# Other start addresses for the operand tiles of the second projections

## The chip, the cores and the metric

The kernel runs on one core of one Trainium2 chip. The metric is the time of one launch on the device, in microseconds. The kernel before was run three times: 2399.58, 2400.55 and 2401.14 us, median 2400.55 us.

## The reference

A small diffusion backbone in float32 takes 512 latent tokens and 256 context tokens (768 in all) of width 1024 through two layers. Each layer is a half-step SwiGLU, a token mixer (a gated short convolution in layer 0, grouped attention in layer 1) and another half-step SwiGLU. That makes six sub-layers. Each has an RMSNorm with a shift and a scale ahead, and a gated residual behind:

```python
def swiglu(h, w_in, w_out):
    gate, up = jnp.split(h @ w_in, 2, axis=-1)          # 1024 -> 2 x 2816
    return (jax.nn.silu(gate) * up) @ w_out             # 2816 -> 1024
def short_conv_mixer(h, w_in, w_conv, w_out):
    b_gate, c_gate, v = jnp.split(h @ w_in, 3, axis=-1)
    u = c_gate * v
    ...
    return (b_gate * y) @ w_out                         # 1024 -> 1024
```

The last product of each sub-layer, `... @ w_out`, is the **second projection**. Everything else is the first.

## The kernel before

**Layout.** Features lie on the 128 partitions and tokens along the free axis. A float32 operand is kept as two parts, high (`h`) and low (`l`), and a product is made of three matmuls (`mm3`, L875 to L878): high weights with high data (L876), high weights with low data (L877), low weights with high data (L878). So along a run of matmuls the moving operand goes high, low, high, high, low, high. Each matmul has its own weight load in front of it.

**First projections.** The SwiGLUs and the convolution compute most of them with Strassen-like products, seven per chunk of 128 features, on half the tokens each (384). Their data operands are the tiles `tB11`, `tB21`, `tB22`, `tT1` to `tT4`, each as `h` and `l`, in numbered slots. A product has 12 matmuls of 384 columns (4 blocks of 128 features, three matmuls each). The order of the products is fixed by `product_order`, and PE and SP follow the program's order.

**Second projections.** What the first projection of a chunk gives is split into `gh` and `gl` (ACT writes the high part, L205, VectorE the low part, L206). The SwiGLU takes its 22 chunks in six parts, one of two chunks and five of four (`FFN_PARTS`), the convolution its eight chunks in two parts of four. When a part is complete, `out_steps` (or, for the last part of the first three sub-layers, `out_close`) multiplies it into eight blocks of 128 output features. The tokens are taken as 512 and then 256, in `out_close` as 384 and 384. Over both groups a part of four chunks is 8 x 4 x 3 x 2 = 192 matmuls, and one of two chunks is 96.

**The tiles of the change.** `gated` (L1084, called by `g_of` and `z_of`) makes four tiles per part in the pool `g0`: tag `G0` holds the high parts of chunks 0 and 1, `G1` the high parts of chunks 2 and 3, `G2` the low parts of chunks 0 and 1, `G3` the low parts of chunks 2 and 3. One tile is two chunks of 768 float32 numbers, 6144 bytes per partition. Each tag has one buffer, which the next part fills again. A tag gets its place in the pool when it is first asked for. In the kernel before that happens in the boot, with a raw weight tile in `G0` and then weight tiles named `late` in `G2`, `G1` and `G3`, so the places stand in the order G0, G2, G1, G3. The pool `g0` serves the first four sub-layers (both SwiGLUs and the convolution of layer 0, the first SwiGLU of layer 1). The attention and the last SwiGLU have pools of their own.

Other users of these tags are `fT3` in `G1` and `fT4` in `G3` (sums that VectorE makes for the first projection) and the `late` weights of the boot. Behind `g0` in memory lie the pool `qp` (what the first projections give on the way to `gh` and `gl`) and the tiles `aw` of the modulation weights.

Of the kernel before, what the change touches and what calls it, by code (L numbers as in the profile page):

```python
# [10 lines left out]
F32 = mybir.dt.float32  # L11
# [7 lines left out]
P = 128  # L19
# [7 lines left out]
NH = NT // 2  # L27
# [106 lines left out]
def backbone(ctx: ExitStack, tc: tile.TileContext, a: dict, out: bass.AP):  # L134
# [25 lines left out]
    @contextmanager  # L160
    def psum(**tags):
        with ExitStack() as st:
            for tag, n in tags.items():
                pool = st.enter_context(tc.tile_pool(name=f"ps{tag}", bufs=n, space=PSUM))
                for t in tag:
                    bank[t] = pool, tag
            yield
# [1546 lines left out]
        return go  # L1714

    with tc.tile_pool(name="apool", bufs=1) as apool, tc.tile_pool(name="g0", bufs=1) as gp, tc.tile_pool(name="qp", bufs=1) as qp, psum(A=3, B=1, C=3, S=1):
        stage["ssq"] = lambda: apool.tile([P, 2, 512], F32, name="ssq", tag="acc").rearrange("p a b -> p (a b)")
        one, two = TOKENS

# [190 lines left out]
```

## Time and profile before

| what | value |
|---|---|
| median of three runs | 2400.55 us |
| the profiled execution | 2400.25 us |
| its span, first to last instruction | 2398.4 us |
| granted TensorE clock, mean | 0.998 |
| VectorE busy | 2031.9 us, 85% of the span |
| ScalarE (ACT) busy | 1166.3 us, 49% |
| GpSimd (POOL) busy | 135.4 us, 6% |
| DMA read from HBM | 249.16 MB |

A matmul is pipelined: the profile gives it a duration of about 390 ns for 512 columns, but the next one starts about 227 ns after it. So durations of matmuls are not the cost of one. What one costs in a run without gaps is the distance between two starts, which the timeline shows to 0.01 us. PEld is the weight load, which runs beside the matmuls. An address is given below as its remainder by 128 bytes.

### The profile page before, as it was taken

The numbers are of one execution on the slowest core, as the hardware profiler recorded it, in microseconds if no ns is written. First come the engines' busy times: TensorE is split into PE (matmuls) and PEld (weight loads), VectorE is DVE, ScalarE is ACT, GpSimd is POOL, SyncE is SP. The second block draws the span as 40 slices with busy tenths as digits, with TensorE's granted clock in tenths as the row PEclk, the third lists the DMA queues.
The fourth block names the chain that finished last, engine by engine and source line by source line (L and its number), as shares of the span: only waits on it lengthen the run. The fifth ranks groups of instructions, "written<-read, shape, count | busy, mean of one in ns | idle before, by whom it ended". The sixth has DMA issues, their size and how long they took to land.

```text
span 2398.4 us, 37639 instructions
## 1 busy us (share of the span) xinstructions
PE 2377.5 (99%) x14303; PEld 2252.4 (94%) x14303; DVE 2031.9 (85%) x4018; ACT 1166.3 (49%) x2198; POOL 135.4 (6%) x256
## 2 busy tenths in 40 slices
PE   9999999999999999999999999999999999999998
PEld 6999999999999999999999999999998889999998
DVE  6989989978988888888877988788778987987777
ACT  5634334355535553443435544343356776555555
POOL 0001111100000001000000001101100000000000
PEclk9999999999999999999999999999999999999999
DMA  9234444430334123323432144444441101233331
GB/s 337 86 113 139 129 127 131 129 115 27 107 105 132 40 70 116 119 95 117 128 105 67 51 130 129 142 139 120 136 132 54 45 10 58 70 121 96 99 106 62
DMA packets 93062, 253.71 MB, mean 106 GB/s; under 512 B 10320, under 2 KB 18640, under 8 KB 92880
## 3 DMA queue, kind: packets, MB, share of 16 engines
q1 hardware_dynamic: 71984, 183.65, 23.7%
q0 software_dynamic: 20352, 67.12, 9.5%
q8 instruction: 112, 1.84, 0.3%
q14 instruction: 70, 0.57, 0.1%
q10 hardware_dynamic: 544, 0.52, 0.1%
HBM read 249.16 MB, written 2.10 MB: 105 GB/s over the span
## 4 chain that ended last, share of the span: by engine, by line
PE 91%; DVE 4%; ACT 3%; DMA 1%; issue 1%; SPq 0%; DVEq 0%; ACTq 0%
PE ps_A L876 16%; PE ps_A L877 16%; PE ps_A L878 16%; PE ps_C L877 11%; PE ps_C L878 11%; PE ps_C L876 11%; PE ps_B L878 3%; PE ps_B L877 3%; PE ps_B L876 3%; PE ps_T L1557 1%; DVE f L778 0%; DMA ada<-in_ada_w 0%; DMA raw<-in_ffn_w_in 0%; ACT pr L1540 0%; PE ps_O L878 0%
## 5 line engine op out<-in xcount | busy, mean ns | idle before, releaser
L205 ACT ACTIVATE w<-raw 128x512 fp32r<-128x512 f32 (+1 forms) x862 | 522.4, 619 | 713.6 <-PE ps_A L878 222.6
L206 DVE TENSOR_TENSOR w<-raw,w 128x512 fp32r<-128x512 f32 (+1 forms) x862 | 574.0, 678 | 120.0 <-ACT w L205 106.3
L525 POOL DMA_DIRECT2D aw<-in_ada_t x240 | 129.4, 539 | 1367.0 <-DVE mods L546 968.5
L389 DVE TENSOR_TENSOR raw<-raw,raw 128x512 f32<-128x512 f32 x264 | 181.4, 688 | 10.0 <-DMA raw<-in_ffn_w_in 6.0
L877 PE MATMUL ps_C<-gl,w 128*128 128x512 f32 (+1 forms) x548 | 188.3, 344 | 0.0
L876 PE MATMUL ps_C<-gh,w 128*128 128x512 f32 (+1 forms) x548 | 188.1, 343 | 0.0
L878 PE MATMUL ps_C<-gh,w 128*128 128x512 f32 (+1 forms) x548 | 188.0, 343 | 0.0
L876 PE MATMUL ps_A<-gh,w 128*128 128x512 f32 (+1 forms) x540 | 185.5, 344 | 0.6 <-DVE x L944 0.6
L877 PE MATMUL ps_A<-gl,w 128*128 128x512 f32 (+1 forms) x540 | 185.6, 344 | 0.0
L878 PE MATMUL ps_A<-gh,w 128*128 128x512 f32 (+1 forms) x540 | 185.4, 343 | 0.0
L546 DVE CUSTOM_DVE_ANT_0 ps_S<-aw,silu_row,packed 128x512 f32<-128x512 f32 x208 | 156.8, 754 | 2.1 <-DMA aw<-in_ada_t 0.8
L546 DVE CUSTOM_DVE_ANT_0 ps_S<-aw,silu_row,mods 128x512 f32<-128x512 f32 x208 | 156.7, 753 | 1.0
L944 DVE SCALAR_TENSOR_TENSOR x<-ps_C,gat,x 128x512 f32<-128x512 f32 (+1 forms) x158 | 99.4, 630 | 44.0 <-PE ps_C L878 43.6
L876 PE MATMUL ps_A<-tB11h,w 128*128 128x384 f32 (+1 forms) x400 | 129.6, 324 | 0.2 <-ACT tB11h L800 0.2
L877 PE MATMUL ps_A<-tB11l,w 128*128 128x384 f32 (+1 forms) x400 | 129.3, 323 | 0.2 <-DVE tB11l L801 0.2
L878 PE MATMUL ps_A<-tB11h,w 128*128 128x384 f32 (+1 forms) x400 | 129.2, 323 | 0.0
L878 PE MATMUL ps_C<-tB22h,w 128*128 128x384 f32 (+2 forms) x376 | 121.6, 323 | 0.0
L877 PE MATMUL ps_C<-tB22l,w 128*128 128x384 f32 (+2 forms) x376 | 121.4, 323 | 0.0
L876 PE MATMUL ps_C<-tB22h,w 128*128 128x384 f32 (+2 forms) x376 | 121.3, 323 | 0.0
L944 DVE SCALAR_TENSOR_TENSOR x<-ps_A,gat,x 128x512 f32<-128x512 f32 (+1 forms) x162 | 101.7, 637 | 16.6 <-PE ps_A L878 16.4
L876 PEld LDWEIGHTS ps_A<-gh,w 128*128 128x128 f32 x540 | 102.2, 189 | 14.1 <-issue 1.0
L878 PEld LDWEIGHTS ps_C<-gh,w 128*128 128x128 f32 x548 | 103.8, 189 | 12.3
(486 smaller groups left out, 6938.7 us busy)
## 6 DMA issues: line engine op xcount, KB each, us to landing
raw<-in_ffn_w_in SPq DMA_DIRECT2D x170, 512.0 KB, 3.7
aw<-in_ada_t POOLq DMA_DIRECT2D x240, 256.0 KB, 2.9
raw<-in_ffn_w_out SPq DMA_DIRECT2D x80, 512.0 KB, 3.9
raw<-in_conv_w_in SPq DMA_DIRECT2D x24, 512.0 KB, 3.6
ada<-in_ada_w SPq DMA_DIRECT2D x28, 256.0 KB, 5.3
raw<-in_attn_w_qkv SPq DMA_DIRECT2D x12, 512.0 KB, 4.7
raw<-in_ada_w SPq DMA_DIRECT2D x8, 512.0 KB, 6.6
silu_row<-in_crow POOLq DMA_DIRECT2D x8, 512.0 KB, 4.1
```

The source lines that it names most:

```text
L205: hi = act.activation(dsth, src, AF.Copy)
L206: lo = dve.tensor_tensor(out=dstl, in0=src, in1=dsth.bitcast(F32), op=ALU.subtract)
L389: dve.tensor_tensor(out=quad(o), in0=quad(x), in1=quad(y), op=ALU.subtract)
L525: nc.gpsimd.dma_start(w, a["ada_t"][t, kh, j])
L546: ins = dve.tensor_tensor_reduce(out=junk, in0=w, in1=silu_row[kh][:, v, :], scale=1.0, scalar=total if kh else ada_b[:, i, hm // 2, col : ...
L876: pe.matmul(ps, wh, xh, start=first, stop=False, **kw)
L877: pe.matmul(ps, wh, xl, start=False, stop=False, **kw)
L878: pe.matmul(ps, wl, xh, start=False, stop=last, **kw)
L944: dve.scalar_tensor_tensor(out=x, in0=p[:, o - off : o - off + w], scalar=gat[:, m, v : v + 1], in1=x, op0=ALU.mult, op1=ALU.add)
L1557: pe.transpose(pt[:, c, :], pr[:, (c0 + c) * P : (c0 + c + 1) * P], ident)
```

## The change

Two lines are added ahead of everything that asks the pool `g0` for a tile:

```diff
     with tc.tile_pool(name="apool", bufs=1) as apool, tc.tile_pool(name="g0", bufs=1) as gp, ...
+        for tag, words in (("G0", 4 * NH + 16), ("G2", 4 * NH), ("G1", 4 * NH + 16), ("G3", 4 * NH)):
+            gp.tile([P, words], F32, name=f"place{tag}", tag=tag)
         stage["ssq"] = lambda: ...
```

`NH` is 384, so `4 * NH` words are the 6144 bytes of before. Two tags get 16 words (64 bytes) more than is used. Nothing reads or writes the placing tiles. The built program has the same instructions in the same order, with the same waits, on every engine; only the source lines behind L1716 move by two, and these start addresses differ:

| tile (bytes per partition) | start before, remainder by 128 | start now, remainder by 128 |
|---|---|---|
| `G0`: high parts of chunks 0, 1 | 184928, 96 | 184928, 96 |
| `G2`: low parts of chunks 0, 1 | 191072, 96 | 191136, 32 |
| `G1`: high parts of chunks 2, 3; `fT3` | 197216, 96 | 197280, 32 |
| `G3`: low parts of chunks 2, 3; `fT4` | 203360, 96 | 203488, 96 |
| tiles of `qp` and `aw` | | all 128 further up |

A chunk within a tile, and a token group within a chunk, begins a multiple of 128 bytes behind the tile's start, so the remainder of the tile holds for each matmul that reads it. All slots of the first projections, all weight tiles of the ring `w` and those held for the last part lie at remainder 96, before and now. Before, every moving operand of a second projection did too. Now the high and the low part of one chunk differ by 64.

One tile set of the kernel before has other remainders: in the first sub-layer `tB22` (and `tB12`) has rows of 386 numbers instead of 384 (two more columns for a shift), 1544 bytes, so that its four blocks of features begin at 96, 104, 112 and 120.

## The prediction

> **What bounds the kernel now.** I read the page first: the share of the engines, and the chain of work that ended last.
>
> ```profile
> span 2398.4 us, 37639 instructions
> ...
> PE 2377.5 (99%) x14303; PEld 2252.4 (94%) x14303; DVE 2031.9 (85%) x4018; ACT 1166.3 (49%) x2198; POOL 135.4 (6%) x256
> ...
> PE 91%; DVE 4%; ACT 3%; DMA 1%; issue 1%; SPq 0%; DVEq 0%; ACTq 0%
> ```
>
> PE is busy for 99% of the span and is 91% of the chain. Then the waits of PE, longest first:
>
> ```profile
> engine line waited for: us in total, times, longest us
> PE ps_C L500 <- DMA ada<-in_ada_w: 4.5, 1, 4.5
> PE ps_S L510 <- ACT adr L506: 0.9, 2, 0.6
> PE ps_T L1557 <- DVE p L206: 0.9, 3, 0.4
> PE ps_A L876 <- DVE x L944: 0.6, 1, 0.6
> ```
>
> The longest is 4.5 us in the boot. The one in a second projection (the last row) is 0.6 us, once, and no row names `gh` or `gl`. So the time is the number of matmuls times the distance between two starts, and only that distance is at stake. I therefore read the timeline of PE in a second projection of the first sub-layer, of which these are the first and last rows of two runs (start, duration, then the tiles):
>
> ```profile
> start us, us, engine line op out<-in xcount [idle before <-releaser]
> 245.24 0.39 PE L878 MATMUL ps_A<-gh,w 128*128 128x512 f32 x1
> ...
> 252.04 0.39 PE L878 MATMUL ps_A<-gh,w 128*128 128x512 f32 x1
> ...
> 252.62 0.28 PE L876 MATMUL ps_C<-gh,w 128*128 128x256 f32 x1
> ...
> 254.42 0.28 PE L876 MATMUL ps_C<-gh,w 128*128 128x256 f32 x1
> ```
>
> There are 30 steps from the first to the second row: 6.80 us / 30 = 226.7 ns for 512 columns. There are 15 steps from the third to the fourth: 1.80 / 15 = 120 ns for 256. The difference is 106.7 ns for 256 columns, so 0.417 ns per column. What is left, 120 - 106.7 = **13.3 ns, is a fixed part of each step**. The columns must be streamed whatever their address, unless the rate itself changes. So the fixed part is what a start address can most plausibly touch.
>
> **How many matmuls the change reaches.** This is counted from the loops and confirmed by a view of the stages that takes the instructions on `gh` alone:
>
> ```profile
> core 0: us, PE busy (x) PEld busy (x) DVE busy (x) ACT busy (x), PEclk, DMA share, GB/s
> 244.08:277.30 33.22, 31.13 (x128) 21.81 (x128) 0.56 (x1) 0.52 (x1) 1.00 0.40 120
> ```
>
> 128 matmuls on `gh` and so 64 on `gl` make the 192 of a part of four chunks. Three SwiGLUs with five such parts and one of 96, and the convolution with two parts, give 3 x (5 x 192 + 96) + 2 x 192 = 3552 matmuls. Of these, per four chunks, 64 read the high and 32 the low part of chunks 0 and 1, and as many those of chunks 2 and 3. Sorted by tile: 1280 stay in place (high, 0 and 1), 640 + 1088 = **1728 begin 64 bytes further up** (low of 0 and 1, high of 2 and 3), 544 begin 128 further up. At 1422 steps the remainder goes from 96 to 32 and at as many back, so 2844 steps lead between unlike remainders. Before there was none.
>
> **The cost of each part.** No instruction, wait or DMA is added, removed or moved, so everything depends on the price of an address. The trace has no operand moved by 64, so I bound the price by the nearest rows.
>
> First bound, from above. In the first sub-layer the rows of `tB22` are 8 bytes longer, and nine of the 12 matmuls of its product begin at remainders 104, 112 and 120 instead of 96. From one such product to the next lie seven products, 84 matmuls. I take three of these periods in the first sub-layer, and three in the second SwiGLU, where all begin at 96:
>
> ```profile
> 198.27 0.33 PE L876 MATMUL ps_C<-tB22h,w 128*128 128x384 f32 x1
> ...
> 241.99 0.33 PE L876 MATMUL ps_C<-tB22h,w 128*128 128x384 f32 x1
> ```
>
> ```profile
> 956.64 0.33 PE L876 MATMUL ps_C<-tB22h,w 128*128 128x384 f32 x1
> ...
> 1000.32 0.33 PE L876 MATMUL ps_C<-tB22h,w 128*128 128x384 f32 x1
> ```
>
> 43.72 against 43.68 us: 0.04 us for three products, 13.3 ns each, for 27 displaced matmuls **1.5 ns each** (0.7 to 2.2 with the rows' last digit). So an address does matter here, by little. For 1728 matmuls that is +2.6 us (at most 3.8).
>
> Second bound, from below. In the boot, one modulation product is computed from two groups of four weight tiles, the first at remainder 96 (`ada`), the second at 0 (`awb`):
>
> ```profile
> 46.01 1.06 PE L500 MATMUL ps_B<-ada,silu_p 128*32 128x512 f32 x8
> 47.01 0.45 PE L876 MATMUL ps_A<-tB21h,w 128*128 128x384 f32 x1
> ```
>
> ```profile
> 48.28 1.07 PE L500 MATMUL ps_B<-awb,silu_p 128*32 128x512 f32 x8
> 49.27 0.45 PE L876 MATMUL ps_A<-tB21h,w 128*128 128x384 f32 x1
> ```
>
> 1.00 us against 0.99 for eight records: -1.2 ns each, with the last digit from -3.7 to +1.2. At worst that is 1728 x -3.7 = -6.4 us. These matmuls are of another kind (32 weight columns, float32).
>
> The value I take is **nothing**. The second row, which moves by 32 bytes, gives nothing that its digits can tell. The first is nearer in kind, but its displacements are odd multiples of 8 bytes in two of three cases, and 1.5 ns would still be only 0.1% of the time.
>
> [...]
>
> The 544 matmuls moved by 128 keep their remainder: nothing. Bounded by the same 1.5 ns they cost 0.8 us. 72 matmuls of the boot whose weights lie in the `late` tiles at remainder 32 are worth 0.1 us at most.
>
> The writers of the moved tiles are ACT and VectorE, here VectorE's:
>
> ```profile
> L206 DVE TENSOR_TENSOR gl<-g,gh x158: 418/552/561, 122.9 to 2366.2; 128x384 fp32r<-128x384 f32 x118, 128x256 fp32r<-128x256 f32 x40
> ```
>
> Should a write take longer, 118 of 552 ns are 65 us in all, so 1% is 0.7 us, spread over four sub-layers and lying beside PE, which never waits for `gl` in the rows above. If that cover were gone, the 0.7 us would show. The tiles of `qp` and `aw` move by 128 and are read and written off PE's path; GpSimd, which loads `aw`, spends most of its time waiting for room:
>
> ```profile
> L525 POOL DMA_DIRECT2D aw<-in_ada_t x240 | 129.4, 539 | 1367.0 <-DVE mods L546 968.5
> ```
>
> The sum against the profiled execution is 2400.25 + 0. This run lies 0.3 us under the median of 2400.55, so I write 2400.5. Its own range, with the two bounds, is 2394 to 2404.5.
>
> **The rivals.**
>
> Slower: *a step between unlike remainders costs.* The 13.3 ns that a product on `tB22` takes longer may not come from nine displaced matmuls but from the one step per product that leads back, from 120 to 96. The change makes 1422 steps back, from 96 to 32 at a low part or the next chunk. At 13.3 ns they give 18.9 us: 2419.5. For it: the product has just one such step, and the excess is as large as the fixed part. Against it: three rows in the page of time cannot tell this from a cost spread over all nine. It decides from 4.8 / 1422 = 3.4 ns per step on.
>
> Faster: *high and low at the same remainder stand in each other's way, and the fixed part is the price.* Before, each operand begins at the same place as the one ahead of it and as the weights loaded beside it. If half of the 13.3 ns went at the 2844 unlike steps, that would be 6.7 x 2844 = 19.0 us: 2381.5. For it: the fixed part is there at every width, and every pair in the kernel is alike. Against it: nine displaced matmuls on `tB22` have weights at another remainder than their data, and took longer, not shorter.
>
> [...]
>
> That the change does not do what it says is excluded: the addresses in the built program differ as given, and nothing else does.
>
> **How the numbers follow.** About 0.2% (4.8 us) is what a measurement of this kernel can tell from no change. Forecast, no visible effect: 0.54. The slower rival, with a price per step anywhere from 3.4 to 13.3 ns: 0.28. The faster one, from 4.8 to 19 us: 0.18. I give the slower one more because the only displaced products in the trace are slower. The predicted time is 2400.5 us. For 8 in 10 the range must take in the forecast's 2394 to 2404.5 and, on each side, what leaves at most about a tenth: of the slower cases (4.8 to 19 us, evenly) those up to +14.5, leaving 0.09; of the faster ones those to -11.5, leaving 0.09. So 2389 to 2415.
>
> **What the changed profile would show.** The rows of the timeline at a second projection decide. If 30 steps at 512 columns are again 6.80 us and 15 at 256 again 1.80, the forecast is right. If the slower rival holds, the distances go up at the steps from 96 to 32 (high to low part in chunks 0 and 1, low to high in 2 and 3), by 13 ns at most, and the last sub-layer, whose pool did not move, stays as it is. If the faster rival holds, the same steps get shorter. In each case the product on `tB22` and the first projections keep their distances. A difference elsewhere, or PE waits on `gh` or `gl`, would say that my reading by PE alone is wrong; a streaming rate that changes with the address, with a loss that grows with the columns, would break the limit by the fixed part.

## The result and the profile after

| | median, us | lowest to highest | runs |
|---|---|---|---|
| before | 2400.32 | 2399.40 to 2401.14 | 22 |
| changed | 2403.37 | 2402.94 to 2404.11 | 22 |

The changed kernel takes 3.05 us longer, a ratio of 1.0013 with a 95% interval of 1.0008 to 1.0019. That is within 0.2%, but the two sets of runs don't overlap: it is slower. The prediction's 2400.5 us was 2.9 us too low, and its range of 2389 to 2415 held the time.

The page of the changed kernel, at the lines that the prediction showed of before:

```profile
span 2401.8 us, 37639 instructions
...
PE 2380.8 (99%) x14303; PEld 2249.8 (94%) x14303; DVE 2032.4 (85%) x4018; ACT 1165.9 (49%) x2198; POOL 135.0 (6%) x256
...
PE 90%; DVE 4%; ACT 3%; DMA 2%; issue 1%; SPq 0%; DVEq 0%; ACTq 0%
```

The span is 3.4 us longer and PE's busy time 3.3 us, with the same number of instructions everywhere. The waits of PE in the changed kernel are these:

```profile
PE ps_C L500 <- DMA ada<-in_ada_w: 4.7, 2, 4.5
PE ps_S L510 <- ACT adr L506: 1.0, 2, 0.7
PE ps_T L1557 <- DVE p L206: 0.9, 3, 0.4
...
PE ps_A L876 <- DVE x L944: 0.6, 1, 0.6
```

They are those of before to 0.2 us, again without `gh` or `gl`. So no wait of more than that was added, and what grew is the distance between matmuls that run without a gap. The timeline of PE in the changed kernel, at the four places that the prediction read (the same part of the first sub-layer, 30 steps from the first row to the second and 15 from the third to the fourth):

```profile
start us, us, engine line op out<-in xcount [idle before <-releaser]
245.55 0.39 PE L878 MATMUL ps_A<-gh,w 128*128 128x512 f32 x1
...
252.51 0.40 PE L878 MATMUL ps_A<-gh,w 128*128 128x512 f32 x1
...
253.10 0.28 PE L876 MATMUL ps_C<-gh,w 128*128 128x256 f32 x1
...
254.86 0.28 PE L876 MATMUL ps_C<-gh,w 128*128 128x256 f32 x1
```

At 512 columns 6.96 us / 30 = 232.0 ns, where it was 226.7. At 256 columns 1.76 / 15 = 117.3 ns, where it was 120. **One width got slower and the other faster.** A second place, in the second SwiGLU of layer 0, shows the same over whole runs. The rows are the first matmul at 512 columns, the first at 256, the next at 512, and the first of the product that follows the part; there are 36, 36 and 120 steps between them. Before:

```profile
910.80 0.39 PE L876 MATMUL ps_C<-gh,w 128*128 128x512 f32 x1
...
919.00 0.28 PE L876 MATMUL ps_C<-gh,w 128*128 128x256 f32 x1
...
923.32 0.40 PE L876 MATMUL ps_A<-gh,w 128*128 128x512 f32 x1
...
944.16 0.34 PE L876 MATMUL ps_A<-tB11h,w 128*128 128x384 f32 x1
```

Changed:

```profile
912.35 0.39 PE L876 MATMUL ps_C<-gh,w 128*128 128x512 f32 x1
...
920.68 0.28 PE L876 MATMUL ps_C<-gh,w 128*128 128x256 f32 x1
...
924.91 0.39 PE L876 MATMUL ps_A<-gh,w 128*128 128x512 f32 x1
...
945.85 0.34 PE L876 MATMUL ps_A<-tB11h,w 128*128 128x384 f32 x1
```

The first run of 512 went from 8.20 to 8.33 us, the first of 256 from 4.32 to 4.23, the whole part from 33.36 to 33.50. I measured every stage of both traces in this way, from its first matmul to the first of the next stage. The second projections of the first four sub-layers are 2.89 us longer in sum: +0.175 for each part of four chunks in the first sub-layer and +0.142 in the others. By width, the 2.89 us are +5.63 at 512 columns (1488 matmuls), +0.53 at 384 (576) and -3.28 at 256 (1488), which is +3.8, +0.9 and -2.2 ns per step: **the change gains at 256 columns and loses more than that at 512.** The last sub-layer is the same to 0.01 us. What remains of the 3.4 us is about 0.5, spread over many stages; the largest pieces are the attention (+0.15) and the boot (+0.13), and +0.018 stands in the first matmuls behind most parts.

### The profile page after: what moved, and what is told of

It is laid out like the page before. It is cut to its first block, busy times and chain, and to the rows that moved or that the text cites. A ratio compares the mean times of both kernels' runs of the same rounds, so it can differ in the third digit from the quotient of the medians.

```text
span 2401.8 us, 37639 instructions
## 1 busy us (share of the span) xinstructions
PE 2380.8 (99%) x14303; PEld 2249.8 (94%) x14303; DVE 2032.4 (85%) x4018; ACT 1165.9 (49%) x2198; POOL 135.0 (6%) x256
## 4 chain that ended last, share of the span: by engine, by line
PE 90%; DVE 4%; ACT 3%; DMA 2%; issue 1%; SPq 0%; DVEq 0%; ACTq 0%
PE ps_A L876 16%; PE ps_A L878 16%; PE ps_A L877 16%; PE ps_C L878 10%; PE ps_C L876 10%; PE ps_C L877 10%; PE ps_B L878 3%; PE ps_B L876 3%; PE ps_B L877 3%; DMA ada<-in_ada_w 1%; PE ps_T L1557 1%; DVE f L778 0%; DMA raw<-in_ffn_w_in 0%; ACT pr L1540 0%; PE ps_O L878 0%
## 5 line engine op out<-in xcount | busy, mean ns | idle before, releaser
L389 DVE TENSOR_TENSOR raw<-raw,raw 128x512 f32<-128x512 f32 x264 | 181.7, 690 | 8.8 <-DMA raw<-in_ffn_w_in 4.4
```

Source lines behind the costliest of these rows:

```text
L389: dve.tensor_tensor(out=quad(o), in0=quad(x), in1=quad(y), op=ALU.subtract)
```

## The experiments

Every address is told here by one number: **d, the start of the data tile less the start of the weight tile, in bytes, by its remainder by 256.** The weights that the second projections read begin at 96 by 256. Before, d is 0 for all four tiles. The table gives d in the order high and low of chunks 0 and 1, then high and low of chunks 2 and 3. "Part" is what a part of four chunks takes longer than before (33.34 us in the first sub-layer, 33.35 in the second SwiGLU of layer 0), and "sum" the same for all second projections of the first four sub-layers. Both are read from the traces. Each median is compared with that of the kernel before, run beside it (2400.32 us for the change, 2400.07 to 2400.10 for the others).

| kernel | d | median, us | ratio [95%] | part: first, later | sum |
|---|---|---|---|---|---|
| the change | 0, 64, 64, 128 | 2403.37 | 1.0013 [1.0008, 1.0019] | +0.175, +0.142 | +2.89 |
| `e1_all_at_32` | 64, 64, 64, 64 | 2397.65 | 0.9990 [0.9981, 0.9999] | -0.484, -0.065 | -2.72 |
| `e2_pairs_apart` | 0, 0, 64, 64 | 2402.27 | 1.0010 [1.0001, 1.0019] | +0.125, +0.124 | +2.16 |
| `e3_whole_lines` | 0, 128, 128, 128 | 2405.17 | 1.0021 [1.0013, 1.0030] | +0.195, +0.221 | +4.66 |
| `e4_lows_at_32` | 0, 64, 128, 192 | 2405.03 | 1.0021 [1.0012, 1.0030] | +0.302, +0.281 | +5.08 |
| `e5_everything_64` | 0, 0, 0, 0 | 2399.99 | 1.0000 [0.9991, 1.0009] | 0.00, 0.00 | 0.00 |
| `e6_long_rows_of_B22` | 64, 64, 64, 64 | 2394.23 | 0.9976 [0.9967, 0.9986] | -0.484, -0.500 | -6.74 |
| `e7_by_256` | 0, 0, 0, 0 | 2400.39 | 1.0001 [0.9992, 1.0010] | 0.00, 0.00 | -0.01 |
| `e8_all_by_128` | 128, 128, 128, 128 | 2408.49 | 1.0035 [1.0023, 1.0048] | +0.407, +0.441 | +8.07 |
| `e9_all_by_192` | 192, 192, 192, 192 | 2401.44 | 1.0006 [0.9997, 1.0015] | +0.346, -0.074 | +0.98 |
| `e10_late_T_64` | 64, 64, 64, 64 | 2391.05 | 0.9961 [0.9949, 0.9974] | -0.484, -0.500 | -6.75 |
| `e11_one_low_tile` | 0, 64, 0, 0 | 2402.30 | 1.0010 [1.0001, 1.0019] | +0.076, +0.049 | +1.89 |
| `e12_weights_moved` | 64, 64, 64, 64 (not in the last parts) | 2394.56 | 0.9976 [0.9966, 0.9986] | -0.049, -0.073 | -1.09 |
| `e13_change_long_rows` | 0, 64, 64, 128 | 2404.10 | 1.0017 [1.0008, 1.0027] | +0.175, +0.159 | +3.12 |
| `e14_lows_at_64` | 0, 64, 0, 64 | 2404.48 | 1.0018 [1.0009, 1.0026] | +0.258, +0.244 | +4.12 |

Split by width like the change, the sums of the other kernels have its two signs wherever d is not 0. At 512 and at 256 columns they are +2.00 and -4.73 us with all tiles at 64 (`e1_all_at_32`), +7.62 and -1.09 at 128, +8.15 and -7.61 at 192, +3.62 and -1.80 in `e2_pairs_apart`, +6.37 and -2.58 in `e14_lows_at_64`. So the two signs don't need a mixture of distances, and the time of a kernel is what is left of two larger numbers.

The expectations call the theories by letters. **A**: a step between unlike starts costs. **B**: each matmul whose data stand 64 away from the weights costs. **C**: the tiles behind the pool, which move too, cost. **D**: the distance d of each matmul sets its step, whatever its neighbours are. **E**: the start of the data counts by itself. **F**: the state in which a run is entered persists through it. **G**: neighbours with unlike d throw a run out of its even pattern. The later ones were formed when the earlier ones fell.

### Which part of the change costs

The four kernels of the first round differ from the change in the placing line alone. `e1_all_at_32` puts a pad ahead and moves all four tiles by 64, so that there is no unlike step left:

```diff
-        for tag, words in (("G0", 4 * NH + 16), ("G2", 4 * NH), ("G1", 4 * NH + 16), ("G3", 4 * NH)):
+        for tag, words in (("pad", 16), ("G0", 4 * NH), ("G2", 4 * NH), ("G1", 4 * NH), ("G3", 4 * NH)):
```

> All four operand tiles of the second projections (first four sub-layers) begin 64 bytes further up: every moving operand at remainder 32, none unlike its neighbour. Theory A (a step between unlike remainders has a price; the change has 2844 such steps for 3.05 us, 1.07 ns each): no such step, so as before, 2400.3 us, and in the timeline 6.80 us for 30 steps at 512 columns and 1.80 us for 15 at 256. Theory B (a moving operand at 32 beside weights at 96 has a price; the change has 1728 for 3.05 us, 1.77 ns each): all 3552 have it, +6.3 us, 2406.6.

Measured: 2397.65 us, 2.45 faster than before. A had 2400.3 and missed this gain. B fell: the most displaced kernel is the fastest of this round. Its rows in the second SwiGLU of layer 0:

```profile
909.44 0.39 PE L876 MATMUL ps_C<-gh,w 128*128 128x512 f32 x1
...
917.69 0.28 PE L876 MATMUL ps_C<-gh,w 128*128 128x256 f32 x1
...
921.93 0.39 PE L876 MATMUL ps_A<-gh,w 128*128 128x512 f32 x1
...
942.73 0.34 PE L876 MATMUL ps_A<-tB11h,w 128*128 128x384 f32 x1
```

8.25 us at 512 columns (+0.05) and 4.24 at 256 (-0.08): the same two signs as in the change, in another proportion.

`e2_pairs_apart` keeps high and low of a chunk together and moves chunks 2 and 3 by 64:

```diff
+        for tag, words in (("G0", 4 * NH), ("G2", 4 * NH + 16), ("G1", 4 * NH), ("G3", 4 * NH)):
```

> Chunks 0 and 1 at remainder 96 (high and low), chunks 2 and 3 at 32 (high and low). Theory A: unlike steps only from chunk to chunk, about 540 of them, +0.6 us, 2400.9. Theory B: 1632 matmuls at 32, +2.9 us, 2403.2, close to the change.

Measured: 2402.27 us, the sum +2.16, between what A (2400.9) and B (2403.2) gave. There are a fifth as many unlike steps as in the change (two per 12 matmuls of a part of four chunks, at most 2 x 272 = 544, against 2844), and three quarters of its loss. A single price per unlike step is out: 2.89 us / 2844 = 1.0 ns in the change, 2.16 / 544 = 4.0 ns here at the least.

`e3_whole_lines` moves all tiles but the first by 128, `e4_lows_at_32` each by 64 more than the one ahead:

```diff
+        for tag, words in (("G0", 4 * NH + 32), ("G2", 4 * NH), ("G1", 4 * NH), ("G3", 4 * NH)):
```

```diff
+        for tag, words in (("G0", 4 * NH + 16), ("G2", 4 * NH + 16), ("G1", 4 * NH + 16), ("G3", 4 * NH)):
```

> Low parts of chunks 0 and 1 and both tiles of chunks 2 and 3 move by 128 bytes, and what lies behind them too: every remainder by 128 is as before. Theories A and B: as before, 2400.3. If it is the moved tiles of qp and aw, or any move at all, that costs (theory C): as the change, 2403.4.

> High parts of all chunks at 96, low parts of all chunks at 32. Theory A: 2368 unlike steps (to each low part and back), +2.5 us, 2402.8. Theory B: 1184 matmuls at 32, +2.1 us, 2402.4. This run alone doesn't tell A from B by the time; by the timeline A lengthens the steps around the low part and leaves the one from high to high alone, B lengthens those of the low part alone.

Measured: 2405.17 and 2405.03 us. A and B missed both: they had 2400.3 for the first, and 2402.8 and 2402.4 for the second. In `e3_whole_lines` every remainder by 128 is as before, and yet it loses more than the change. Either it was the tiles behind the pool (C), or addresses count by more than 128.

### By what an address counts

Four kernels to tell C, D and E apart. `e5_everything_64` places nothing and moves everything, data and weights, by 64:

```diff
-SHIFT = 24
+SHIFT = 40
```

> The places of the change are gone, and instead every tile of the kernel in SBUF begins 64 bytes further up, weights and data alike, so that data and weights still begin at the same remainder by 256. Theory D (the distance between a data start and a weight start sets the step): as before, 2400.1 us, steps of 120, 173.3 and 226.7 ns. Theory E (the start of the data itself sets it): as with the four tiles at the new place, so steps near 230 ns at 512 columns and 113 to 118 at 256 in the second projections, and changed steps in the first projections as well.

`e7_by_256` is `e3_whole_lines` with 256 bytes for 128, and `e8_all_by_128` moves all four tiles by 128:

```diff
+        for tag, words in (("G0", 4 * NH + 64), ("G2", 4 * NH), ("G1", 4 * NH), ("G3", 4 * NH)):
```

```diff
+        for tag, words in (("pad", 32), ("G0", 4 * NH), ("G2", 4 * NH), ("G1", 4 * NH), ("G3", 4 * NH)):
```

> High parts of chunks 0 and 1 in place, the three other tiles 256 bytes further up. Theories D and E with a period of 256 bytes: as before, 2400.1 us, every distance in the timeline as before. If any unlike start costs whatever its size: as the run by 128 or the change, 2403 to 2405.

> All four tiles 128 bytes up, so that no two neighbours are unlike. In the run by whole 128 one tile stayed and three moved, +5.1 us. If unlike neighbours are the cause (theory A at a period of 256): as before, 2400.1. If the distance of data and weights sets the price (theory D): all 3552 matmuls pay what 2272 paid there, about +8 us, 2408.

Measured: 2399.99 us, 2400.39 and 2408.49. A common move does nothing, which speaks against E. A move by 256 does nothing, although the tiles behind the pool move by it, which speaks against C. (`e11_one_low_tile` below ends it: there too they stand 256 up, and it loses.) A move of all four tiles by 128 costs 8.4 us, with no unlike step in it, so A alone falls. The rows of `e7_by_256` and then of `e8_all_by_128`:

```profile
911.09 0.39 PE L876 MATMUL ps_C<-gh,w 128*128 128x512 f32 x1
...
919.29 0.28 PE L876 MATMUL ps_C<-gh,w 128*128 128x256 f32 x1
...
923.61 0.40 PE L876 MATMUL ps_A<-gh,w 128*128 128x512 f32 x1
```

```profile
915.14 0.40 PE L876 MATMUL ps_C<-gh,w 128*128 128x512 f32 x1
...
923.54 0.28 PE L876 MATMUL ps_C<-gh,w 128*128 128x256 f32 x1
...
927.82 0.40 PE L876 MATMUL ps_A<-gh,w 128*128 128x512 f32 x1
...
948.94 0.34 PE L876 MATMUL ps_A<-tB11h,w 128*128 128x384 f32 x1
```

8.20 and 4.32 us in the first, to the digit those of before. 8.40 and 4.28 in the second.

`e12_weights_moved` has the placing lines of `e1_all_at_32` and puts a tile of 48 words (192 bytes) ahead of the ring of weights. The weights move by 192. The four tiles, which lie behind the ring, move by 192 + 64 = 256, so that by 256 they begin where they did before. That makes d = 64 with the weights moved in place of the data:

```diff
+    wp.tile([P, 48], F32, name="placew", tag="placew", bufs=1)
```

> The data tiles begin at the remainders by 256 of before; the ring of the weights is moved by 192, so that data stand 64 above the weights in first and second projections alike (in the parts whose weights lie in slots, and the second projections of the last sub-layer, the distance is 0 as before). Theory D: the second projections as in the first run (parts of four -0.07 or -0.48 us), the products of 384 columns about as before (those parts of 384 columns did not change there), the products of 256 columns in the last sub-layer 113 to 118 ns instead of 120: 2386 to 2393. Theory E (the data's own start): as before, 2400.1.

Measured: 2394.56 us, less of a gain than D gave (2386 to 2393), but far from E's 2400.1. In the later sub-layers a part is 0.073 us shorter, where moving the data had given 0.065: with the data at their remainder of before, the weights alone do it. E is out, and in these kernels d by 256 is what an address counts by. Two things differ from `e1_all_at_32`, since the first projections read the same ring, while their data stand still, and get d = 64 too. The first sub-layer's parts gain 0.049 instead of 0.484, and in the last sub-layer each stage of 336 first-projection matmuls of 256 columns is 0.735 us shorter. Most of this kernel's gain lies there: 3.55 us in the first projections of the last sub-layer, against the sum of 1.09. Where the weights of a last part stand in slots, which didn't move, d is another. It stays 0 in those of the first three sub-layers and in three quarters of that of the fourth. In the last sub-layer it is 192, and the 132 matmuls of 256 columns that begin its last part are 0.868 us shorter, 6.6 ns each, as in the later sub-layers of `e9_all_by_192` below (113.5 ns for 119.8).

`e9_all_by_192` moves all four tiles by 192, with `("pad", 48)` for `("pad", 16)`:

> All four tiles 192 bytes up, none unlike its neighbour: the fourth distance of data and weights by 256 (0 is the kernel before, 64 gave -2.5 us, 128 gave +8.4). Theory D says only that the second projections of the first four sub-layers take another length and the last sub-layer the same; if the four distances lie on one wave, the one at 192 mirrors that at 64, some -2 us, 2398. Theory A: 2400.1.

Measured: 2401.44 us, a miss by 3.4. A distance of 192 is the mirror image of 64 only in the later sub-layers (-0.074 against -0.065). In the first it costs 0.346 where 64 gains 0.484. And the likeness of -0.074 and -0.065 is chance: the first run at 512 columns and the one at 256 behind it take 8.39 and 4.09 us here, 8.25 and 4.24 in `e1_all_at_32`.

### What the first sub-layer has

In `e1_all_at_32` a part gains 0.484 us in the first sub-layer and 0.065 in the others, at equal d. What differs is the product ahead of it: only in the first sub-layer does `tB22` have rows of 386 numbers. `e6_long_rows_of_B22` gives every sub-layer of that width such rows (the two more columns aren't multiplied):

```diff
+        if name == "B22" and geo.half == NH:
+            more = 2
...
-                    mm3(ps, wh[:, k, :], wl[:, k, :], xh[:, k, :], xl[:, k, :], kh == 0 and k == 0, kh == 1 and k == 3)
+                    mm3(ps, wh[:, k, :], wl[:, k, :], xh[:, k, : ps.shape[-1]], xl[:, k, : ps.shape[-1]], kh == 0 and k == 0, kh == 1 and k == 3)
```

> All four tiles 64 bytes up as in the first run, and tB22 gets its rows of 386 numbers in the next two sub-layers and the first SwiGLU of layer 1 too, where they were 384, so that the product ahead of each second projection is like that of the first sub-layer. In the first run a part of four chunks was shorter than before by 0.48 us in the first sub-layer, but by 0.07 in the two other SwiGLUs. Theory F (the state in which the run of matmuls is entered persists through it): the parts of the other SwiGLUs become shorter by 0.48 too where that product stands ahead of them, four per SwiGLU, -0.42 each, -3.3 us in all, against some +0.5 us for the products on the long rows: 2394.9. If the state is not carried over, they stay at -0.07 and the time is that of the first run or 0.5 above, 2397.7 to 2398.2.

Measured: 2394.23 us, 3.4 less than `e1_all_at_32`. A part of a later sub-layer gains 0.500, as the first one's do, for 0.047 us that the long rows cost in each stage of first projections ahead of it. Its rows (the lines of this kernel stand two further down):

```profile
908.44 0.39 PE L878 MATMUL ps_C<-gh,w 128*128 128x512 f32 x1
...
916.68 0.28 PE L878 MATMUL ps_C<-gh,w 128*128 128x256 f32 x1
...
920.76 0.39 PE L878 MATMUL ps_A<-gh,w 128*128 128x512 f32 x1
...
941.29 0.34 PE L878 MATMUL ps_A<-tB11h,w 128*128 128x384 f32 x1
```

The gain sits at 256 columns: 4.08 us for 36 steps, 113.3 ns, against 4.24 in `e1_all_at_32` with the same d and the same instructions in that run. So **what happened ahead of this run decided its steps**: F holds here. The run at 512 columns ahead of it hardly differs in length (8.24 us against 8.25). There the steps of the three matmuls that `mm3` makes are about 226, 229 and 232 ns in turn in both kernels, by the starts in the traces. In `e6_long_rows_of_B22` the 226 lies behind the first of the three, in `e1_all_at_32` behind the third, and in the first sub-layer of `e1_all_at_32`, where 256 columns take 113.3 ns too, behind the first again.

`e13_change_long_rows` puts the same edit on top of the change, since F could also be why the change loses:

> The change itself, and tB22 with rows of 386 numbers in all SwiGLUs and the convolution, as in the run that took -0.5 us off each part of four when all tiles stood at one distance. Theory G (unlike neighbours keep throwing the run out of its pattern, so nothing of the state at its entry lasts): the parts stay where the change has them, +0.14 to +0.18 us each, and the long rows cost some 0.9 us: 2404 to 2404.5. If the entry decides the pattern here too: parts some 0.4 us shorter, eight of them, 2401.

Measured: 2404.10 us, the later parts +0.159. The entry, which made 0.435 us a part at equal distances (-0.065 to -0.500), does next to nothing where distances are mixed (0.017 us a part).

### Whether the mixture costs

By D alone the change is the sum of its tiles. With the sums of the kernels whose tiles all have one d (64: -2.72 us, 128: +8.07, for 3552 matmuls), 1728 matmuls at 64 and 544 at 128 give -1.32 + 1.24 = -0.1 us, where +2.89 was measured. `e11_one_low_tile` leaves one tile at 64 and brings the others to 0, and `e14_lows_at_64` does so with both low tiles:

```diff
+        for tag, words in (("G0", 4 * NH + 16), ("G2", 4 * NH + 48), ("G1", 4 * NH), ("G3", 4 * NH)):
```

```diff
+        for tag, words in (("G0", 4 * NH + 16), ("G2", 4 * NH + 48), ("G1", 4 * NH + 16), ("G3", 4 * NH)):
```

> Only the low parts of chunks 0 and 1 stand 64 bytes off; the tiles of chunks 2 and 3 are 256 bytes up, which is as before. If each matmul pays by its own distance (theory D, summed): 640 of 3552 matmuls at 64, -0.4 us, 2399.7. If neighbours at unlike distances throw the run out of its even steps (theory G): 1280 unlike steps of the change's 2844, +1.4 us, 2401.5, all of it at chunks 0 and 1 and shortly behind them.

> Only two distances, alternating in every chunk: high parts 0, low parts 64 from the weights (chunks 2 and 3 lie 256 further up, which is as before). Theory D, summed over matmuls: 1184 at 64, -0.8 us, 2399.3. Theory G: twice the unlike steps of the run with one low tile, which had +2.2 us: about +4 us, 2404.

Measured: 2402.30 and 2404.48 us. D gave 2399.7 and 2399.3; G gave 2401.5 and about 2404. With d = 0 throughout the kernel takes 2400.1, with d = 64 throughout 2397.65, and with the two in turn 2404.48. **Of 0 and 64 neither costs, and their mixture does.** It does so at 512 columns, by 6.37 us against 0 and 2.00. At 256 the mixture (-2.58) lies between the two (0 and -4.73). G fits the place of the loss, at 512 columns, but not its size: a part of the later sub-layers loses five times as much in `e14_lows_at_64` as in `e11_one_low_tile`, not twice, and the matmuls of 384 columns lose 0.34 us against 0.86, so the about 2404 was met by chance. `e11_one_low_tile` has a mixed and an unmixed half within one run. Its first 18 steps at 512 columns belong to chunks 0 and 1, high at 0 and low at 64, the next 18 to chunks 2 and 3, both at 0:

```profile
913.36 0.39 PE L876 MATMUL ps_C<-gh,w 128*128 128x512 f32 x1
...
917.53 0.39 PE L876 MATMUL ps_C<-gh,w 128*128 128x512 f32 x1
...
921.62 0.28 PE L876 MATMUL ps_C<-gh,w 128*128 128x256 f32 x1
```

Mixed, 4.17 us / 18 = 231.7 ns, near the changed kernel's 232.0; unmixed, 4.09 / 18 = 227.2. Before, the two halves took 4.12 (910.80 to 914.92) and 4.08:

```profile
914.92 0.39 PE L876 MATMUL ps_C<-gh,w 128*128 128x512 f32 x1
```

What a single change of distance does is seen in `e2_pairs_apart`. Its first run in the second SwiGLU of layer 0 has 18 steps at d = 0 and then 18 at 64. The rows are its 10th matmul, the 19th (the first at 64), the 23rd, and the first at 256 columns:

```profile
913.83 0.39 PE L876 MATMUL ps_C<-gh,w 128*128 128x512 f32 x1
...
915.87 0.40 PE L876 MATMUL ps_C<-gh,w 128*128 128x512 f32 x1
...
916.81 0.39 PE L877 MATMUL ps_A<-gl,w 128*128 128x512 f32 x1
...
920.01 0.28 PE L876 MATMUL ps_C<-gh,w 128*128 128x256 f32 x1
```

Nine settled steps at 0 take 2.04 us (226.7 ns each), the four behind the change of distance 0.94 (some 234), and the 14 that follow at 64 take 3.20 (228.6, near the 228.9 of `e1_all_at_32`). So at 512 columns this run needed some four steps after the change of distance until it had settled again. In the change the distance changes at four of five steps.

### A faster version

`e10_late_T_64` is `e6_long_rows_of_B22` with the gain of `e12_weights_moved` in the last sub-layer: its tiles of first-projection operands begin 64 bytes further up too.

```diff
+        if geo.half < NH:
+            T[name] = [slot(n, [16 + 4 * geo.half], f"t{name}{z}")[:, 16:].rearrange("p (k n) -> p k n", k=4) for n, z in zip(geo.t_slots[name], "hl")]
+            return
```

> The kernel with long rows of tB22, and in the last sub-layer the tiles of the first projections (256 columns) begin 64 bytes further up in their slots, so 64 from the weights. Theory D: the steps of some 1700 matmuls of 256 columns go from 120 ns to 113.3 or 117.3, as those of the second projections did in the first run, -4.6 to -11 us: 2383 to 2390. If it matters only in second projections: 2394.2.

Measured: 2391.05 us, 9.0 less than before, the fastest of all kernels here. The expected size was missed: 3.2 us less than `e6_long_rows_of_B22`, where steps of 113.3 ns would have given more. The stage of 336 matmuls of 256 columns, before and then in this kernel (whose lines stand five further down):

```profile
2142.93 0.28 PE L876 MATMUL ps_A<-tB11h,w 128*128 128x256 f32 x1
...
2183.25 0.40 PE L876 MATMUL ps_C<-gh,w 128*128 128x512 f32 x1
```

```profile
2136.00 0.28 PE L881 MATMUL ps_A<-tB11h,w 128*128 128x256 f32 x1
...
2175.57 0.40 PE L881 MATMUL ps_C<-gh,w 128*128 128x512 f32 x1
```

40.32 us became 39.57: 120.0 and 117.8 ns per step, close to the 117.3 that the changed kernel shows at this width, not 113.3.

## Why the prediction was wrong

**What bounds the kernel** was read rightly. PE stays at 99% busy, no wait of more than 0.2 us came in, and the loss is a distance between starts. The 2.89 us lie in the 3552 matmuls that were counted, and the last sub-layer and, but for 0.018 us behind a part, the first projections kept their times, as the prediction said.

**The step that failed** is "The value I take is **nothing**". It had two bounds. The first, 1.5 ns per displaced matmul from the long rows of `tB22`, came to +2.6 us; the measured value is +3.05 for the time and +2.89 for the matmuls. The second, from weight tiles of another kind of matmul, gave nothing to be told, and that one was followed, although the text itself called the first nearer in kind. Taking the nearer row would have given 2400.5 + 2.6 = 2403.1 us. That would have been luck: the price isn't one per displaced matmul, neither on `tB22` (see the slower rival) nor here, since displacing all 3552 by 64 gains 2.45 us and by 128 costs 8.4. No run bears out the value of nothing: what the runs show in its place is a gain of 3.28 us at 256 columns and a loss of 5.63 at 512. Most of that loss goes with the mixture: the distances alone would give some 2.1 us there, an estimate from the sums of the kernels at one distance (2.00 x 1728 / 3552 + 7.62 x 544 / 3552). The 0.2% below which the prediction expected to see nothing was too coarse as well: the 22 runs of each kernel lie within 1.0 us of their median, so 3 us are plain.

**"The 544 matmuls moved by 128 keep their remainder: nothing"** was wrong as well. The text told addresses by 128, and here they count by 256 and from the weights: a move by 256 left 2400.39 us (`e7_by_256`), one of all four tiles by 128 gave 2408.49 (`e8_all_by_128`), and one of data and weights together by 64 left 2399.99 (`e5_everything_64`). The 128 isn't what the change mainly lost by, though: `e14_lows_at_64`, with 0 and 64 alone, loses more than the change.

**The fixed part.** The argument "The columns must be streamed whatever their address, unless the rate itself changes" fixed the attention on the 13.3 ns of each step. At 512 columns the excess over 0.417 ns per column went up by 5.3 ns (232.0 less 226.7), at 256 down by 2.7. A cost with opposite signs at two widths is not a fixed part. Over all second projections it grows with the columns (-2.2, +0.9 and +3.8 ns at 256, 384 and 512); the prediction's last part had named a change with the columns as what would break that limit.

**The slower rival** had the right sign and the right place, steps between unlike neighbours, but its price was far too high: 13.3 ns, decided from 3.4 ns on. The change shows 1.0 ns for each of its 2844 unlike steps. The reading of `tB22` behind it, one step back per product, was right, and the prediction's 1.5 ns for each of nine matmuls was not. In the trace of before, the first eleven steps of such a product take 1907.5 ns in the mean of 19, where even steps give 1906.7. The twelfth, back from 120 to 96, takes 181.7 for 173.3, and the product behind it 4 ns more. In the product that begins at 198.27 us the twelfth shows as 0.18 us for 0.17:

```profile
200.18 0.34 PE L878 MATMUL ps_C<-tB22h,w 128*128 128x384 f32 x1
200.36 0.34 PE L876 MATMUL ps_A<-tB11h,w 128*128 128x384 f32 x1
```

But that price doesn't carry over to steps of 64, and the loss there is no one price per step: `e2_pairs_apart` pays at least 4.0 ns, `e11_one_low_tile` with 1280 unlike steps 1.89 / 1280 = 1.5 ns.

**The faster rival** said that operands at the place of the weights stand in each other's way. In a version that the prediction didn't have, the times at 256 columns agree with it: with all data at 64 from the weights they take 113.3 to 117.8 ns for 120. Those at 512 don't: 228.9 for 227.4. What the prediction held against it, that the displaced matmuls of `tB22` took longer, doesn't hold for all of them: the three at 112 take 517.5 ns, where even steps give 520. The change gets 3.28 us at 256 columns, where all at 64 gets 4.73, and loses it again at 512.

What stays open: what in the hardware makes d count, and why the run at 512 columns in `e2_pairs_apart` took some four steps to settle after the change of distance. The runs show that it is the relation of data and weights (2399.99 us when both move by 64, 2397.65 when the data alone do), and that the entry matters (4.24 and 4.08 us for the same 36 steps), but no row shows a conflict itself. Nor could the pattern into which a run falls be predicted (the misses of `e9_all_by_192`, `e10_late_T_64` and `e12_weights_moved`). The two signs of the change are shown to come from leaving d = 0, as kernels at one distance have them too, and the mixture of 0 and 64 to add at 512 columns.

## What to carry to other kernels

Where PE is the bound and each matmul has its own weight load, place data and weights by intention: measure the distance of their starts by 256 bytes, and keep it alike for all operands of a run, since here the mixture of 0 and 64 was slower than either (2404.48 us against 2400.1 and 2397.65). Alike is not enough: all at 128 is the slowest kernel here (2408.49 us), all at 64 with long rows of `tB22` among the fastest (2394.23), so the distances have to be tried. A price that the nearest row shows should not be set to nothing for being small, and it should be read step by step before it is multiplied: the 13.3 ns of `tB22` stood behind one step, not in nine. A shift should be tried on the whole set of tiles before it is tried on half. Before a price is called one per instruction, read it at two widths: opposite signs, as here -2.2 and +3.8 ns at 256 and 512 columns, say that it is none.

## What the runs showed of the hardware

- **The distance of data and weights by 256 bytes changed the time of the second projections.** With one distance for all of them, their sum is 0 (d = 0), -2.72 us (64), +8.07 (128) and +0.98 (192), with the entry of each kernel as it is (-6.74 at 64 with long rows of `tB22`). A common move of 64 (`e5_everything_64`, 2399.99 us) and a move by 256 (`e7_by_256`, 2400.39) leave the time within 0.4 us of the kernel before. `e12_weights_moved`, where the weights moved and the data kept their remainder by 256, changed the steps: a part of the later sub-layers became 0.073 us shorter.
- **A change of distance was paid over several steps at 512 columns.** In `e2_pairs_apart` the four steps behind it take some 234 ns, between stretches of 226.7 and 228.6.
- **At 256 columns the weight loads took 192 ns with d = 0 and 187 to 189 with other distances.** These are the medians in the same part of the first sub-layer: 192 before, 188 in `e6_long_rows_of_B22`, which is faster, and 187 to 189 in the changed kernel, which is slower. So their length doesn't explain which is faster.
- **What stood ahead of a run changed its steps where all tiles had one distance.** In `e1_all_at_32` and `e6_long_rows_of_B22` the same matmuls at the same d took 4.24 and 4.08 us for 36 steps, depending on two more columns per row in a product ahead of them. Where the distances are mixed, the same two columns changed a later part by 0.017 us (`e13_change_long_rows`).
